# Last layer's first MLP product: pairs of units as seven products of half the features by half the tokens

## The chip, the cores and the metric

The kernel runs on one NeuronCore of a Trainium2 chip. The metric is the device time of one execution in microseconds (us). TensorE (PE) multiplies, ScalarE (ACT) applies functions and copies, VectorE (DVE) does elementwise arithmetic, SyncE (SP) issues the DMA transfers, and PSUM holds what PE writes.

## The reference, cut to what matters

A block with attention, pooling and convolution branches and an MLP is run for two layers. In the last layer only the 512 latent tokens go through the MLP, whose first product (1024 to 4096 features) is what changes:

```python
D_MODEL = 1024
SEQ = 512
D_FF = 4 * D_MODEL

def squared_relu_mlp(h, w1, w2):
    a = jax.nn.relu(h @ w1)
    return (a * a) @ w2

x = x + mod_x[5] * squared_relu_mlp(modulate(rmsnorm(x, g_norm2[l]), mod_x[3], mod_x[4]),
                                    w_ff1[l], w_ff2[l])
```

## The kernel before, in words

Activations lie with features on the 128 partitions and tokens on the free axis: `T` = 768 columns, of which the first 256 (`CT`) are context tokens and unused in the last layer. `h2` is the normalized input of the MLP, eight feature blocks of 128, each as a pair of float32r tiles, high part `hh` and low part `hl`, whose sum is the full value. Every product is made of three terms: weight high by `hh`, weight high by `hl`, weight low by `hh`.

The 4096 hidden features are 32 units of 128. A unit (`ff1`) loads its weights (`wload`: two DMAs of 128x512, each split by an ACT copy into the high part and a DVE subtraction into the low part), runs 8 feature blocks x 3 terms = 24 matmuls into one PSUM tile `mm` (`dense`), and then takes relu (ACT, out of PSUM), square (ACT) and the split into `ah` and `al` (ACT, DVE). The first eight units are done in two parts of 256 tokens, while the normalization of the second part is still under way; the other 24 units use all 512 tokens, so their matmuls have 512 columns. `ff2` multiplies eight units' results by the second weight matrix: 8 output blocks for each of four chunks, each with 24 matmuls of 512 columns and one DVE addition into `x_cur`.

PSUM tiles `mm` have 1024 columns (two halves of 512) and there are two of them in rotation. Weights have four slots in each of two pools (`wf`, `wb`), raw loads six slots in four pools (`rf`, `pd`, `tf`, `rb`). What stands in which order on each engine is not written by hand: `Plan` records every operation with a cost, lays them out in a list by these costs, with the program's dependencies and the slots, and replays them in that order; the tile framework then adds the semaphore waits. In the plan's own bookkeeping a PSUM operand is taken by halves of 512 columns; the framework adds its waits by its own.

All instructions are recorded by one helper, so the profile gives line 352 for every one and is read by tile names.

Of the kernel before, what the change touches and what calls it, by code (L numbers as in the profile page):

```python
# [9 lines left out]
F32 = mybir.dt.float32  # L10
F32R = mybir.dt.float32r
I32 = mybir.dt.int32
AF = mybir.ActivationFunctionType
ALU = mybir.AluOpType
# [3 lines left out]
CT = 256  # L18
T = 768
# [344 lines left out]
def tile_block(ctx, tc, xT, ccol, wmod, cols, rows, wqkv, wcq, wckv, wuq, wukv, wpool,  # L364
# [3 lines left out]
    V, S, PE = _Rec(plan, 'DVE', nc.vector), _Rec(plan, 'ACT', nc.scalar), _Rec(plan, 'PE', nc.tensor)  # L368
    G, SP = _Rec(plan, 'POOL', nc.gpsimd), _Rec(plan, 'SP', nc.sync)
# [8 lines left out]
    rbp = pool("rb", NB['rb'])  # L378
    rfp = pool("rf", NB['rf'])
    wbp = pool("wb", NB['wb'])  # L380
    wfp = pool("wf", NB['wf'])
    epool = pool("e", NB['e'])
    tpool = pool("tmp", NB['tmp'])
    tfp = pool("tf", NB['tf'])
    pdp = pool("pd", NB['pd'])
    stp = pool("st", 3)
    nwp = pool("nw", 1)
    mcp = pool("mc", 1)
    wmp = pool("wm", 2)
# [8 lines left out]
    def nm(s):  # L398
        uid[0] += 1
        return f"{s}_{uid[0]}"  # L400

    def g_tile(shape=(128, T), n="g"):
        return gpool.tile(list(shape), F32R, tag="g", name=nm(n))

    def tmp(shape=(128, T), n="tmp"):
        return tpool.tile(list(shape), F32, tag="tmp", name=nm(n))
# [7 lines left out]
    def mm():  # L414
        return pmm.tile([128, 1024], F32, tag="mm", name=nm("mm"))
# [40 lines left out]
    def split_to(hi, lo, src):  # L456
        S.activation(hi, src, AF.Copy)
        V.tensor_tensor(out=lo, in0=src, in1=hi, op=ALU.subtract)
# [71 lines left out]
    def mod_chunk(l, ch):  # L530


        nv = 2 if l < DEPTH - 1 or ch < 2 else 1
        for hf in range(4):
            acc = mcp.tile([128, 2, 256], F32, tag="mc", name=nm("macc"))
            for k2 in range(8):
                raw = wmp.tile([128, 1, 256], F32, tag="wm", name=nm("wm"))
                j0 = ch * 1024 + hf * 256
                SP.dma_start(raw[:, 0], wmod[l, k2 * 128:(k2 + 1) * 128, j0:j0 + 256])
                for k in range(1):  # L540
                    kt = k2 + k
                    for v in range(nv):
                        if kt == 0:
                            if TOG[2]:
                                S.activation(acc[:, v], raw[:, k], AF.Copy, scale=silu[:, kt, v:v + 1])
                            else:
                                V.tensor_scalar(acc[:, v], raw[:, k], silu[:, kt, v:v + 1], None, op0=ALU.mult)
                        else:
                            V.scalar_tensor_tensor(out=acc[:, v], in0=raw[:, k], scalar=silu[:, kt, v:v + 1], in1=acc[:, v],
                                                   op0=ALU.mult, op1=ALU.add)  # L550
                if k2 == 3:
                    yield
            pt = pst(512)
            for v in range(nv):
                for j in range(2):
                    PE.transpose(pt[:, v * 256 + j * 128:v * 256 + (j + 1) * 128], acc[:, v, j * 128:(j + 1) * 128], ident)
            for v in range(nv):
                V.tensor_reduce(mods[l][:, 8 * ch + 2 * hf:8 * ch + 2 * hf + 2, v],
                                pt[:, v * 256:(v + 1) * 256].rearrange("p (a b) -> p a b", b=128), axis=AX.X, op=ALU.add)
            if hf == 3:  # L560
                mod_bias(l, ch, nv)
            yield
# [14 lines left out]
    def segs(full):  # L577
        return ([(0, CT, 1)] if full else []) + [(CT, T, 0)]
# [10 lines left out]
    def etile():  # L589
        return epool.tile([128, T], F32, tag="e", name=nm("e"))  # L590
# [51 lines left out]
    def tables(l):  # L642
        rw = tmp((128, NROW), "rw")
        SP.dma_start(rw, rows[l:l + 1, :].partition_broadcast(128))
        ra = tmp((128, 2, 6, 64), "ra")
        SP.dma_start(ra, rope_a)
        rb = tmp((128, 2, 6, 32), "rb")
        SP.dma_start(rb, rope_b)
        V.tensor_scalar(rw[:, R_GQA:R_GQA + 64], rw[:, R_GQA:R_GQA + 64], 0.125, None, op0=ALU.mult)
        V.tensor_scalar(rw[:, R_GQB:R_GQB + 96], rw[:, R_GQB:R_GQB + 96], float(96 ** -0.5), None, op0=ALU.mult)  # L650
        for tc_, ts_, ro, gains, hd in ((TAC, TAS, ra, (R_GQA, R_GKA), 32), (TBC, TBS, rb, (R_GQB + 64, R_GKB + 64), 16)):
            for i, r0 in enumerate(gains):
                def bc(o, n, nt):
                    return rw[:, r0 + o:r0 + o + n].unsqueeze(1).to_broadcast([128, nt, n])
                V.tensor_tensor(out=tc_[:, i], in0=ro[:, 0], in1=bc(0, 2 * hd, 6), op=ALU.mult)
                V.tensor_tensor(out=ts_[:, i, :, 0:hd], in0=ro[:, 1, 2:6, 0:hd], in1=bc(hd, hd, 4), op=ALU.mult)
                V.tensor_tensor(out=ts_[:, i, :, hd:2 * hd], in0=ro[:, 1, 2:6, hd:2 * hd], in1=bc(0, hd, 4), op=ALU.mult)
        V.tensor_tensor(out=gno, in0=rw[:, R_GQB:R_GQB + 64], in1=rw[:, R_GKB:R_GKB + 64], op=ALU.mult)
        sm = st()
        for i in range(2):  # L660
            a = R_LAM + 128 * i
            V.tensor_tensor(out=rw[:, a:a + 64], in0=rw[:, a:a + 64], in1=rw[:, a + 64:a + 128], op=ALU.mult)
            V.tensor_reduce(sm[:, i:i + 1], rw[:, a:a + 64], axis=AX.X, op=ALU.add)
        S.activation(sm[:, 2:4], sm[:, 0:2], AF.Exp)
        li = 0.8 - 0.6 * math.exp(-0.3 * l)
        V.tensor_scalar(neglam, sm[:, 3:4], sm[:, 2:3], -li, op0=ALU.subtract, op1=ALU.add)
# [487 lines left out]
    x_cur = []  # L1154
# [13 lines left out]
    for hf, v in ((0, 0), (0, 1), (1, 0), (1, 1)):  # L1168
# [5 lines left out]
        a, b, _ = segs(True)[1 - v]  # L1174
# [4 lines left out]
    for l in range(DEPTH):  # L1179
        full = l < DEPTH - 1  # L1180
# [10 lines left out]
        x_cur = []  # L1191
# [33 lines left out]
        for hp in range(2):  # L1225
            q = a_qk(l, h1, hp, 0, do_fill)
            k = a_qk(l, h1, hp, 1, do_fill)
# [8 lines left out]
        for g in range(2):  # L1236
            q = b_q(l, cq, g, do_fill)
            for i in range(2):
                k, v = b_kv(l, ckv, 2 * g + i, do_fill)
# [16 lines left out]
        for ni, n in enumerate(order):  # L1256
# [14 lines left out]
            for dp in range(4):  # L1271
# [3 lines left out]
                for dd in range(2):  # L1275
                    d = 2 * dp + dd
# [5 lines left out]
                    ps = mm()  # L1282
# [23 lines left out]
        h2 = None  # L1306
        kept = {}
        later = []

        def step():  # L1310

            if later:
                later.pop(0)()
# [8 lines left out]
        for pi, (a, b, v) in enumerate(parts):  # L1322
            for d in (range(8) if pi == 0 else range(7, -1, -1)):
                hi, lo = wkeep(d, wo[l, d], pi)
                ps = mm()
                dense(ps, hi.rearrange("p (k c) -> p k c", c=128), lo.rearrange("p (k c) -> p k c", c=128), 0, mrg, [parts[pi]])
                if pi == 0:
# [3 lines left out]
                                       in1=x_cur[d][:, a:b], op0=ALU.mult, op1=ALU.add)  # L1331
# [3 lines left out]
            h2 = h2 or h_tiles()  # L1335
# [7 lines left out]
        def ff1(f, seg, pi=1):  # L1343
            hi, lo = wkeep(f, wff1[l, f], pi)
            ps = mm()
            dense(ps, hi.rearrange("p (k c) -> p k c", c=128), lo.rearrange("p (k c) -> p k c", c=128), 0, h2, seg)
            a0, a1 = min(x[0] for x in seg), max(x[1] for x in seg)
            a = tmp()
            S.activation(a[:, a0:a1], ps[:, CT + a0:CT + a1], AF.Relu)
            S.activation(a[:, a0:a1], a[:, a0:a1], AF.Square)  # L1350
            if f not in acts:
                acts[f] = (g_tile(n="ah"), g_tile(n="al"))
            split_to(acts[f][0][:, a0:a1], acts[f][1][:, a0:a1], a[:, a0:a1])
            mod_step()
# [3 lines left out]
        def ff2(c, d, seg, pi=1):  # L1358
            hi, lo = wkeep(d, wff2[l, c, d], pi)
            ps = mm()  # L1360
            dense(ps, hi.rearrange("p (k c) -> p k c", c=128), lo.rearrange("p (k c) -> p k c", c=128), 0,
                  [acts[8 * c + k] for k in range(8)], seg)
            for a, b, v_ in seg:
                V.scalar_tensor_tensor(out=x_cur[d][:, a:b], in0=ps[:, CT + a:CT + b], scalar=mods[l][:, 40 + d, v_:v_ + 1],
                                       in1=x_cur[d][:, a:b], op0=ALU.mult, op1=ALU.add)
                if c == 3 and full:
                    acc_square(x_cur[d], ss, d == (0, 7)[pi], a, b)
            mod_step()
            if c == 3 and not full:
                SP.dma_start(out[d], x_cur[d][:, CT:])  # L1370

        if full:
            modq.extend([mod_chunk(l + 1, ch) for ch in range(6)])
        for pi, part in enumerate(parts):
            for f in (range(8) if pi == 0 else range(7, -1, -1)):
                ff1(f, [part], pi)
                step()
        for c in range(3):
            if full and c == 1:
                tables(l + 1)  # L1380
            for f in range(2):
                ff1(8 * (c + 1) + f, segs(full))
            for d in range(8):
                ff2(c, d, segs(full))
            for f in range(2, 8):
                ff1(8 * (c + 1) + f, segs(full))
        if not full:
            for d in range(8):
                ff2(3, d, segs(full))
# [98 lines left out]
```

## Time and profile before

| | us |
|---|---|
| median of 3 runs | 2675.24 (2673.6 to 2675.96) |
| profiled execution, whole | 2676.63 |
| its span, first to last instruction | 2674.9 |
| PE busy in it | 2643.3 (99%) |
| DVE busy | 1754.0 (66%) |
| ACT busy | 1172.6 (44%) |

The sum in the prediction is made on the profiled execution, whose time is 1.7 us over its span and 1.4 us over the median. Busy time of PE is from the start to the modelled end of its matmuls, which overlap; how long one really takes is read from the distance of their starts.

### The profile page before, as it was taken

How to read it: one execution, taken by the hardware profiler on the slowest of the kernel's cores; microseconds unless marked ns; L12 is line 12 of the kernel's file. 1: busy time of each engine (PE TensorE's matmuls, PEld its weight loads, DVE VectorE, ACT ScalarE, POOL GpSimd, SP SyncE). 2: the span in 40 equal slices, each digit the busy share in tenths (PEclk: the TensorE clock that was granted, in tenths of full speed). 3: DMA queues.
4: the chain of work that ended last, by engine and by line, in shares of the span. 5: the costliest groups of instructions: out<-in, count | busy, mean ns of one | idle time of the engine just before them, and what ended most of it. 6: DMA issues, size and time to landing. Idle time of an engine off the chain costs nothing.

```text
span 2674.9 us, 41960 instructions
## 1 busy us (share of the span) xinstructions
PE 2643.3 (99%) x15620; PEld 2310.8 (86%) x15620; DVE 1754.0 (66%) x3978; ACT 1172.6 (44%) x2444; POOL 13.4 (1%) x63
## 2 busy tenths in 40 slices
PE   8999999999999999999999999999999999999999
PEld 4899888989988888988888888888888888988887
DVE  6668666689986778445455467787467887743332
ACT  4355443446564225414141434555455562544332
POOL 0000000000000000000000000000000000000000
PEclk9999999999999999999999999999999999999999
DMA  7222233334446643333444422223232366433332
GB/s 245 77 62 68 87 99 118 96 119 121 130 131 205 213 132 111 103 94 105 127 132 129 127 92 88 72 69 109 89 102 75 94 210 204 147 112 102 95 95 79
DMA packets 189533, 311.90 MB, mean 117 GB/s; under 512 B 21520, under 2 KB 72080, under 8 KB 189328
## 3 DMA queue, kind: packets, MB, share of 16 engines
q1 hardware_dynamic: 189328, 309.22, 37.4%
q8 instruction: 123, 2.02, 0.3%
q14 instruction: 82, 0.67, 0.1%
HBM read 270.86 MB, written 38.27 MB: 116 GB/s over the span
## 4 chain that ended last, share of the span: by engine, by line
PE 92%; DVE 3%; DMA 3%; ACT 1%; issue 1%; SPq 0%; DVEq 0%; ACTq 0%
PE mm L352 79%; PE pst L352 8%; PE sc L352 4%; DMA wmp<-in_wmod_dram 1%; DMA tmp<-y 1%; ACT wh L352 0%; DVE wl L352 0%; DMA wr<-in_wqkv_dram 0%; DVE hl L352 0%; DVE e L352 0%; DMA wm<-in_wmod_dram 0%; DVE ks L352 0%; DVE qd L352 0%; DVE st L352 0%; PE R L352 0%
## 5 line engine op out<-in xcount | busy, mean ns | idle before, releaser
L352 ACT ACTIVATE wh<-wr 128x512 fp32r<-128x512 f32 (+2 forms) x664 | 396.8, 618 | 733.3 <-PE mm L352 608.8
L352 PE MATMUL mm<-hh,wh 128*128 128x256 f32 (+1 forms) x1984 | 613.2, 354 | 2.2 <-DVE xx L352 1.0
L352 PE MATMUL mm<-hh,wl 128*128 128x256 f32 (+1 forms) x1984 | 611.3, 353 | 0.7 <-DVE wl L352 0.6
L352 PE MATMUL mm<-hl,wh 128*128 128x256 f32 (+1 forms) x1984 | 609.7, 353 | 0.0
L352 DVE TENSOR_TENSOR wl<-wr,wh 128x512 fp32r<-128x512 f32 (+2 forms) x664 | 441.7, 676 | 216.6 <-ACT wh L352 210.3
L352 PEld LDWEIGHTS mm<-hh,wl 128*128 128x128 f32 x1984 | 371.4, 189 | 46.4 <-DVE wl L352 1.1
L352 PEld LDWEIGHTS mm<-hh,wh 128*128 128x128 f32 x1984 | 370.6, 189 | 47.2 <-ACT gt L352 1.2
L352 PEld LDWEIGHTS mm<-hl,wh 128*128 128x128 f32 x1984 | 370.7, 189 | 45.5
L352 DVE SCALAR_TENSOR_TENSOR macc<-wm,silu,macc 128x256 f32<-128x256 f32 x448 | 206.1, 481 | 99.3 <-DMA wm<-in_wmod_dram 94.4
L352 PE MATMUL mm<-ah,wh 128*128 128x512 f32 (+1 forms) x768 | 241.9, 355 | 0.4 <-ACT wh L352 0.3
L352 PE MATMUL mm<-al,wh 128*128 128x512 f32 (+1 forms) x768 | 241.8, 355 | 0.0
L352 PE MATMUL mm<-ah,wl 128*128 128x512 f32 (+1 forms) x768 | 241.1, 355 | 0.0
L352 DVE SCALAR_TENSOR_TENSOR xx<-mm,mod,xx 128x256 f32<-128x256 f32 (+1 forms) x96 | 61.3, 660 | 169.7 <-PE mm L352 169.6
L352 ACT ACTIVATE ph<-pst 128x384 fp32r<-128x384 f32 (+1 forms) x216 | 103.2, 478 | 140.8 <-PE pst L352 139.9
L352 PEld LDWEIGHTS mm<-ah,wh 128*128 128x128 f32 x768 | 144.5, 188 | 21.7 <-ACT wh L352 0.8
L352 PEld LDWEIGHTS mm<-al,wh 128*128 128x128 f32 x768 | 144.5, 188 | 21.1 <-issue 0.2
L352 PEld LDWEIGHTS mm<-ah,wl 128*128 128x128 f32 x768 | 144.4, 188 | 20.8 <-issue 0.2
L352 ACT ACTIVATE e<-sc,st 128x768 f32<-128x768 f32 (+1 forms) x160 | 130.5, 815 | 70.9 <-DVE st L352 47.5
L352 PE MATMUL mm<-wh,hh 128*128 128x256 f32 x544 | 154.6, 288 | 2.1 <-ACT wh L352 1.4
L352 PE MATMUL mm<-wl,hh 128*128 128x256 f32 x544 | 154.6, 286 | 0.9 <-DVE wl L352 0.9
L352 PE MATMUL mm<-wh,hl 128*128 128x256 f32 x544 | 153.9, 285 | 0.0
L352 DVE TENSOR_REDUCE st<-sc 128x1 f32<-128x768 f32 (+1 forms) x160 | 135.5, 847 | 19.5 <-PE sc L352 17.0
(196 smaller groups left out, 4579.1 us busy)
## 6 DMA issues: line engine op xcount, KB each, us to landing
wr<-in_wff_dram SPq DMA_DIRECT2D x280, 256.0 KB, 3.0
wr<-in_wdense_dram SPq DMA_DIRECT2D x192, 256.0 KB, 3.0
wm<-in_wmod_dram SPq DMA_DIRECT2D x320, 128.0 KB, 2.2
wr<-in_wbr_dram SPq DMA_DIRECT2D x64, 256.0 KB, 3.6
wr<-in_wqkv_dram SPq DMA_DIRECT2D x48, 256.0 KB, 2.8
g<-gt SPq DMA_DIRECT2D x32, 384.0 KB, 2.6
gt<-g SPq DMA_DIRECT2D x32, 384.0 KB, 3.5
wr<-in_wo_dram SPq DMA_DIRECT2D x48, 256.0 KB, 3.0
```

The lines of the kernel that those rows point to most:

```text
L352: ins = fn(*a, **k).ins
```

## The change

In the last layer the 24 units after the first eight are done in pairs (f, f + 1). A pair is a product of 2 x 2 blocks: the weights are split by unit and by half of the input features (feature blocks 0 to 3 and 4 to 7), the activations by half of the input features and half of the tokens (`lo_t` 256 to 511, `hi_t` 512 to 767). Eight block products become seven, of sums of blocks. `form_sums` makes four sums of activation blocks once: three go where there is room (`t1`, `t2` in the unused context columns of `h2`, `t3` in tiles of other pools) and the fourth is kept in `x_cur` until `form_last` writes it over the block '12'. Each `product` has 4 feature blocks x 3 terms = 12 matmuls of 256 columns into a quarter of a PSUM tile, `pa` or `pb`; `form_w` splits a raw weight block or a sum of them into high and low part. In `ff1_pair` seven sums combine the products into the two units' results, which then take relu, square and split. The order of the calls in a chunk also changes: one pair, six `ff2`, one pair, two `ff2`, two pairs, in place of two units, eight `ff2`, six units.

```diff
+        def form_sums(i, keep4):
+            b11, b12, b21, b22 = (tuple(y[:, t] for y in h2[d]) for d, t in ((i, lo_t), (i, hi_t), (i + 4, lo_t), (i + 4, hi_t)))
+            t1, t2 = (tuple(y[:, free_t] for y in h2[d]) for d in (i, i + 4))
...
+            for dst, b in ((f22, b22), (f12, b12), (f11, b11)):
+                V.tensor_tensor(out=dst, in0=b[0].bitcast(F32), in1=b[1].bitcast(F32), op=ALU.add)
+            V.tensor_tensor(out=t3f, in0=f22, in1=f12, op=ALU.subtract)
+            split_blocks(t3, t3f)
+            V.tensor_tensor(out=f12, in0=f12, in1=f11, op=ALU.subtract)
+            split_blocks(t1, f12)
+            V.tensor_tensor(out=f11, in0=t3f, in1=f11, op=ALU.add)
+            split_blocks(t2, f11)
+            V.tensor_tensor(out=keep4, in0=b21[0].bitcast(F32), in1=b21[1].bitcast(F32), op=ALU.add)
+            V.tensor_tensor(out=keep4, in0=keep4, in1=f11, op=ALU.subtract)
...
+        def form_last(i, keep4):
+            split_blocks(forms['12', i], keep4)
...
+        def product(ps, w, key):
+            for kt in range(4):
+                bh, bl = forms[key, kt]
+                wh, wl = w[:, kt * 128:kt * 128 + 128], w[:, 512 + kt * 128:640 + kt * 128]
+                for i, (w_, b_) in enumerate(((wh, bh), (wh, bl), (wl, bh))):
+                    PE.matmul(ps, lhsT=w_, rhs=b_, start=(kt == 0 and i == 0), stop=(kt == 3 and i == 2))
+
+        def ff1_pair(f):
...
+            pa = mm()
+            pb = mm()
+            p1, p7, p4, p3 = (pa[:, a:a + 256] for a in (0, 512, 256, 768))
+            p6, p5, p2 = (pb[:, a:a + 256] for a in (0, 512, 256))
+            sn = etile()
+            s1, s2, s3 = (sn[:, 256 * k:256 * k + 256] for k in range(3))
+            u1, u2 = tmp(), tmp()
+            product(p1, form_w(r11), '11')
+            S.activation(s1, p1, AF.Copy)
+            V.tensor_tensor(out=r21, in0=r11, in1=r21, op=ALU.subtract)
+            product(p7, form_w(r21), '3')
+            w22 = form_w(r22)
+            V.tensor_tensor(out=r22, in0=r22, in1=r21, op=ALU.subtract)
+            product(p6, form_w(r22), '2')
+            V.tensor_tensor(out=s2, in0=p6, in1=s1, op=ALU.add)
+            V.tensor_tensor(out=s3, in0=p7, in1=s2, op=ALU.add)
+            V.tensor_tensor(out=r11, in0=r22, in1=r11, op=ALU.add)
+            product(p5, form_w(r11), '1')
+            V.tensor_tensor(out=u2[:, hi_t], in0=p5, in1=s3, op=ALU.add)
+            V.tensor_tensor(out=s2, in0=p5, in1=s2, op=ALU.add)
+            product(p4, w22, '12')
+            V.tensor_tensor(out=u2[:, lo_t], in0=p4, in1=s3, op=ALU.add)
+            w12 = form_w(r12)
+            V.tensor_tensor(out=r12, in0=r12, in1=r22, op=ALU.subtract)
+            product(p3, form_w(r12), '22')
+            V.tensor_tensor(out=u1[:, hi_t], in0=p3, in1=s2, op=ALU.add)
+            product(p2, w12, '21')
+            V.tensor_tensor(out=u1[:, lo_t], in0=p2, in1=s1, op=ALU.add)
...
         for c in range(3):
...
+            else:
+                ff1_pair(8 * (c + 1))
+                for d in range(6):
+                    ff2(c, d, segs(full))
+                ff1_pair(8 * (c + 1) + 2)
+                for d in range(6, 8):
+                    ff2(c, d, segs(full))
+                ff1_pair(8 * (c + 1) + 4)
+                ff1_pair(8 * (c + 1) + 6)
```

What the planner made of it is shown at two places. The first is PE where one product ends and the next begins. Before, in the last layer's MLP, this is the seam of a unit of the first product (`hh`, `hl`) and one of the second (`ah`, `al`):

```order
L352 MATMUL mm_4542<-hh_4376,wl_4539 128x512
L352 MATMUL mm_4542<-hh_4378,wh_4538 128x512
L352 MATMUL mm_4542<-hl_4379,wh_4538 128x512
L352 MATMUL mm_4542<-hh_4378,wl_4539 128x512
L352 MATMUL mm_4550<-ah_4432,wh_4546 128x512 [waits Activation_49]
L352 MATMUL mm_4550<-al_4433,wh_4546 128x512 [waits DVE_49]
L352 MATMUL mm_4550<-ah_4432,wl_4547 128x512
```

Every product has a PSUM tile of its own there. In the changed kernel it is the seam of p1 and p7 of the second pair, both in the tile `mm_4597`; `wsf_4602` and `wsf_4603` are their weights (high and low part in one tile), the names that begin with `t_` hold the sum '3':

```order
L352 MATMUL mm_4597<-hh_4370,wsf_4602 128x256
L352 MATMUL mm_4597<-hl_4371,wsf_4602 128x256
L352 MATMUL mm_4597<-hh_4370,wsf_4602 128x256
L352 MATMUL mm_4597<-t_4187_4426,wsf_4603 128x256 [waits Activation_49]
L352 MATMUL mm_4597<-t_4187_4426,wsf_4603 128x256
L352 MATMUL mm_4597<-t_4187_4426,wsf_4603 128x256 [waits Activation_49]
L352 MATMUL mm_4597<-t_4188_4427,wsf_4603 128x256
L352 MATMUL mm_4597<-t_4189_4428,wsf_4603 128x256
```

The first matmul of p7 waits for ACT (the high part of its weights), and so does the third.

The second place is DVE around the readers of PSUM. Before, a stretch of the second product, where each `mm` tile is read once, whole, behind the low parts of weights to come:

```order
L352 SCALAR_TENSOR_TENSOR xx_4309<-mm_4550,mod_133,xx_4309 128x512 [waits PE_49]
L352 TENSOR_TENSOR wl_4567<-wr_4568,wh_4566 128x512 [waits DMAHW3_49,DVE_49,Activation_49]
L352 TENSOR_TENSOR wl_4567<-wr_4569,wh_4566 128x512 [waits DMAHW0_49,Activation_49]
L352 SCALAR_TENSOR_TENSOR xx_4315<-mm_4555,mod_133,xx_4315 128x512 [waits PE_49]
L352 TENSOR_TENSOR wl_4572<-wr_4573,wh_4571 128x512 [waits DMAHW5_49,Activation_49]
L352 TENSOR_TENSOR wl_4572<-wr_4574,wh_4571 128x512 [waits DMAHW2_49,Activation_49]
```

In the changed kernel, in the same second pair, `e_4599` holds s1, s2 and s3, `mm_4598` is `pb`, and `tmp_4601` is u2:

```order
L352 TENSOR_TENSOR wr_4596<-wr_4596,wr_4595 128x512 [waits DVE_49]
L352 TENSOR_TENSOR wl_4619<-wr_4620,wh_4618 128x512 [waits DMAHW5_49,PE_49,Activation_49]
L352 TENSOR_TENSOR wsf_4608<-wr_4596,wsf_4608 128x512 [waits Activation_49]
L352 TENSOR_TENSOR e_4599<-mm_4598,e_4599 128x256 [waits PE_49]
L352 TENSOR_TENSOR e_4599<-mm_4597,e_4599 128x256 [waits DVE_49]
L352 TENSOR_TENSOR wsf_4632<-wr_4623,wsf_4632 128x512 [waits Activation_49]
L352 TENSOR_TENSOR tmp_4601<-mm_4598,e_4599 128x256 [waits DVE_49,PE_49]
L352 TENSOR_TENSOR e_4599<-mm_4598,e_4599 128x256
```

The sums that read `mm` now stand among the weight splits and weight sums, seven times in a pair, and each reads a quarter of a tile.

## Rows read from the trace of the kernel before

**Rows 1.** The page, busy time of each engine.

```profile
PE 2643.3 (99%) x15620; PEld 2310.8 (86%) x15620; DVE 1754.0 (66%) x3978; ACT 1172.6 (44%) x2444; POOL 13.4 (1%) x63
```

**Rows 2.** Windows of the last stage: length, busy times, clock, DMA.

```profile
core 0: us, PE busy (x) PEld busy (x) DVE busy (x) ACT busy (x) POOL busy (x), PEclk, DMA share, GB/s
2365.00:2440.00 75.00, 75.00 (x338) 62.31 (x338) 28.31 (x44) 26.02 (x48) 0.00 (x0) 1.00 0.34 103
2440.00:2520.00 80.00, 80.00 (x355) 66.24 (x354) 29.30 (x44) 27.44 (x49) 0.00 (x0) 1.00 0.31 98
```

**Rows 3.** The chain of waits, 2290 to 2675: its last matmuls.

```profile
2331.29 339.81 PE mm L352 x1637
```

**Rows 4.** Timeline of PE: first and last of 28 matmuls.

```profile
start us, us, engine line op out<-in xcount [idle before <-releaser]
2439.73 0.39 PE L352 MATMUL mm<-hh,wh 128*128 128x512 f32 x1
...
2445.85 0.39 PE L352 MATMUL mm<-hh,wh 128*128 128x512 f32 x1
```

**Rows 5.** Timeline of PE: first and last of 36 matmuls.

```profile
2359.78 0.28 PE L352 MATMUL mm<-hh,wh 128*128 128x256 f32 x1
...
2363.98 0.28 PE L352 MATMUL mm<-hh,wl 128*128 128x256 f32 x1
```

**Rows 6.** Timeline of DVE: operations without a wait between.

```profile
2330.39 1.29 DVE L352 TENSOR_TENSOR wl<-wr,wh 128x512 fp32r<-128x512 f32 x2
2331.59 0.42 DVE L352 TENSOR_TENSOR al<-tmp,ah 128x256 fp32r<-128x256 f32 x1
2331.93 0.87 DVE L352 SCALAR_TENSOR_TENSOR e<-xx,st,R 128x256 f32<-128x256 f32 x2
```

**Rows 7.** Groups of ACT and DVE operations, 2290 to 2675.

```profile
line engine op names shapes xcount | busy us, mean ns | idle before us <-releasers
L352 ACT ACTIVATE wh<-wr 128x512 fp32r<-128x512 f32 x145 | 87.6, 627 | 198.9 <-PE mm L352 194.6 <-DMA wr<-in_wff_dram 4.2
L352 ACT ACTIVATE tmp<-mm 128x256 f32<-128x256 f32 x16 | 6.0, 372 | 2.2 <-PE mm L352 2.2
L352 DVE TENSOR_TENSOR al<-tmp,ah 128x256 fp32r<-128x256 f32 x16 | 6.8, 423 | 3.0 <-ACT ah L352 2.6
```

**Rows 8.** Groups of DVE operations, 2330 to 2365.

```profile
L352 DVE TENSOR_TENSOR wl<-wr,wh 128x512 fp32r<-128x512 f32 x19 | 13.1, 691 | 7.7 <-ACT wh L352 6.9
L352 DVE TENSOR_TENSOR al<-tmp,ah 128x256 fp32r<-128x256 f32 x12 | 5.1, 423 | 2.9 <-ACT ah L352 2.6
L352 DVE SCALAR_TENSOR_TENSOR hl<-e,mod,hh 128x256 fp32r<-128x256 f32 x8 | 3.8, 482 | 0.3 <-ACT hh L352 0.3
```

**Rows 9.** Timeline: PE ends in PSUM, DVE reads it.

```profile
2296.74 0.38 PE L352 MATMUL pss<-ident,ss 128*128 128x128 f32 x2
2297.16 0.42 DVE L352 TENSOR_REDUCE st<-pss 128x2 f32<-128x256 f32 x1 [0.84 <-PE pss L352]
```

**Rows 10.** Timeline: DVE ends, PE restarts on its result.

```profile
1588.26 0.69 DVE L352 TENSOR_TENSOR wl<-wr,wh 128x512 fp32r<-128x512 f32 x1
1589.01 0.39 PE L352 MATMUL mm<-wl,hh 128*128 128x256 f32 x1 [0.90 <-DVE wl L352]
1589.23 0.28 PE L352 MATMUL mm<-wh,hl 128*128 128x256 f32 x1
```

**Rows 11.** Timeline of PE: two stops before the last stage.

```profile
2271.70 0.39 PE L352 MATMUL mm<-ml,wh 128*128 128x256 f32 x1 [0.17 <-DVE ml L352]
2280.08 0.39 PE L352 MATMUL mm<-mh,wh 128*128 128x256 f32 x1 [1.77 <-ACT wh L352]
```

**Rows 12.** Windows with stops of PE.

```profile
1580.00:1590.00 10.00, 7.18 (x53) 6.13 (x51) 9.89 (x21) 4.84 (x10) 0.00 (x0) 1.00 0.00 1
1590.00:1600.00 10.00, 9.69 (x37) 7.51 (x38) 7.95 (x24) 5.12 (x11) 0.00 (x0) 0.83 0.48 158
2268.00:2284.00 16.00, 13.96 (x108) 13.20 (x107) 10.31 (x18) 7.19 (x14) 0.00 (x0) 1.00 0.43 135
```

More of the change, by code (lines that the diff above doesn't have):

```diff
@@ L1370, in ff2, with split_blocks @@
                 SP.dma_start(out[d], x_cur[d][:, CT:])
+        lo_t, hi_t, free_t = slice(CT, 512), slice(512, T), slice(0, CT)
+        forms = {}
+        def split_blocks(blk, src):
+            split_to(blk[0], blk[1], src)
+        def form_sums(i, keep4):
+            b11, b12, b21, b22 = (tuple(y[:, t] for y in h2[d]) for d, t in ((i, lo_t), (i, hi_t), (i + 4, lo_t), (i + 4, hi_t)))
+            t1, t2 = (tuple(y[:, free_t] for y in h2[d]) for d in (i, i + 4))
+            t3 = own3[i]
+            u = etile()
+            w = etile()
+            f22, f12, f11 = (u[:, 256 * k:256 * k + 256] for k in range(3))
+            t3f = w[:, 0:256]
+            for dst, b in ((f22, b22), (f12, b12), (f11, b11)):
[8 more added lines that the diff above has]
+            V.tensor_tensor(out=keep4, in0=keep4, in1=f11, op=ALU.subtract)
+            for n_, b in (('11', b11), ('12', b12), ('21', b21), ('22', b22), ('1', t1), ('2', t2), ('3', t3)):
+                forms[n_, i] = b
@@ new lines, in form_last, with form_w @@
+        def form_last(i, keep4):
+            split_blocks(forms['12', i], keep4)
+        SRAW = ((rfp, "rf"), (pdp, "pd"), (tfp, "tf"), (rbp, "rb"))
+        sturn = [0]
+        def form_w(raw):
+            wp, wt = ((wfp, "wf"), (wbp, "wb"))[sturn[0] % 2]
+            sturn[0] += 1
+            w = wp.tile([128, 1024], F32R, tag=wt, name=nm("wsf"))
+            split_to(w[:, 0:512], w[:, 512:1024], raw)
+            return w
+        def product(ps, w, key):
[4 more added lines that the diff above has]
+                    PE.matmul(ps, lhsT=w_, rhs=b_, start=(kt == 0 and i == 0), stop=(kt == 3 and i == 2))
@@ new lines, in ff1_pair @@
+        def ff1_pair(f):
+            raws = {}
+            for (key, k, a), (rp, rt) in zip((('11', 0, 0), ('21', 1, 0), ('22', 1, 512), ('12', 0, 512)), SRAW):
+                raws[key] = rp.tile([128, 512], F32, tag=rt, name=nm("wr"))
+                SP.dma_start(raws[key], wff1[l, f + k][:, a:a + 512])
+            r11, r21, r22, r12 = (raws[k] for k in ('11', '21', '22', '12'))
+            pa = mm()
[26 more added lines that the diff above has]
+            V.tensor_tensor(out=u1[:, lo_t], in0=p2, in1=s1, op=ALU.add)
+            for k, u in ((1, u2), (0, u1)):
+                S.activation(u[:, CT:T], u[:, CT:T], AF.Relu)
+                S.activation(u[:, CT:T], u[:, CT:T], AF.Square)
+                acts[f + k] = (g_tile(n="ah"), g_tile(n="al"))
+                split_to(acts[f + k][0][:, CT:T], acts[f + k][1][:, CT:T], u[:, CT:T])
@@ L1372, in tile_block @@
         if full:
             modq.extend([mod_chunk(l + 1, ch) for ch in range(6)])
+        else:
+            keep4 = [x_cur[i][:, free_t] for i in range(4)]
+            t3a = mcp.tile([128, 2, 256], F32R, tag="mc", name=nm("t3"))
+            t3b = [wmp.tile([128, 256], F32R, tag="wm", name=nm("t3")) for _ in range(2)]
+            t3c = [g_tile(n="t3") for _ in range(2)]
+            own3 = [(t3a[:, 0], t3a[:, 1]), tuple(t3b)] + [(x[:, 0:256], x[:, 256:512]) for x in t3c]
         for pi, part in enumerate(parts):
@@ L1377, in tile_block @@
                 step()
-        for c in range(3):
[L1379 to L1386, printed above, removed]
+            if pi == 0 and not full:
+                for i in range(4):
+                    later.append(lambda i=i: form_sums(i, keep4[i]))
+        if not full:
+            for i in range(4):
+                form_last(i, keep4[i])
+        for c in range(3):
+            if full:
+                if c == 1:
+                    tables(l + 1)
+                for f in range(2):
+                    ff1(8 * (c + 1) + f, segs(full))
+                for d in range(8):
+                    ff2(c, d, segs(full))
+                for f in range(2, 8):
+                    ff1(8 * (c + 1) + f, segs(full))
+            else:
+                ff1_pair(8 * (c + 1))
[3 more added lines that the diff above has]
+                for d in range(6, 8):
+                    ff2(c, d, segs(full))
+                ff1_pair(8 * (c + 1) + 4)
+                ff1_pair(8 * (c + 1) + 6)
         if not full:
```

## The prediction, made before the changed kernel ran

> **What bounds the kernel now.** Read the page's busy line first [rows 1]: TensorE (PE) is busy 2643.3 of 2674.9 us, but that is a modelled share over many stages, so go to the stage that the change touches. The stretches by windows [rows 2] show the last layer's MLP: PE never idles, VectorE (DVE) works 28 to 29 of 75 to 80 us and ScalarE (ACT) 26 to 27, and the granted clock is 1.00, the 2.4 GHz level. The chain of waits [rows 3] says the same: its last 340 us are one unbroken run of matmuls. So time is gained here only by issuing fewer PE cycles, and lost by every moment in which PE's queue waits. The spacing of matmuls comes from the timeline, by first and last row of an unbroken run: 512 columns take (2445.85 - 2439.73)/27 = 0.227 us [rows 4], 256 columns (2363.98 - 2359.78)/35 = 0.120 us [rows 5]. The "0.39" and "0.28" in those rows are from start to end; neighbours overlap.
>
> **Removed on PE.** Twelve pairs of units change. A pair was 2 x 24 = 48 matmuls of 512 columns, 48 x 0.227 = 10.88 us. It becomes 7 products x 4 feature blocks x 3 terms = 84 matmuls of 256, 84 x 0.120 = 10.08 us. Each pair gives 0.80 us, all twelve 9.6 us. An eighth of the columns goes, but 256-wide matmuls pay their fixed part twice as often.
>
> **Added on DVE and ACT, beside PE.** DVE's 128x512 operations follow one another every 0.60 us, 256-wide ones every 0.34, scalar_tensor_tensor every 0.39 [rows 6] (starts at 2330.39, two operations on at 2331.59, then at 2331.93). A pair now needs 11 of 512 for weights (7 low parts, 4 sums), 7 of 256 to combine products and 2 of 512 for the low parts of the result: 13 x 0.60 + 7 x 0.34 = 10.2 us, against 6 x 0.60 = 3.6 before. For a chunk of four pairs and eight second-matrix units (each 2 x 0.60 and one of 0.75) that is 41 + 16 = 57 us, beside 4 x 10.1 + 8 x 5.44 = 84 us on PE: it fits beside PE, without much to spare where pairs stand back to back. ACT has 7 high parts, one copy and six result operations a pair, 7 x 0.63 + 0.37 + 6 x 0.63 = 8.6 us at the full durations [rows 7], which fits too. I cost both at nothing beyond the waits below. The weights' DMA is four loads of 256 KB a pair, as before; nothing.
>
> **Added once: the sums of activations.** They are 44 + 4 DVE operations of 256, 16.3 us, put into the last eight first-part units (2330 to 2365). There DVE executes 19 operations of 512, 12 of 256 and twice 8 scalar_tensor_tensor [rows 8], about 19 x 0.60 + 12 x 0.34 + 16 x 0.39 = 22 of 35 us; 13 are free, so some 3 to 4.5 us of this work lies behind the seam. The first product needs only plain tokens and the late sums are used by the last products, so the first pair's PE waits little: between 0 and 4.5 us; I take 0.7.
>
> **Added: waits inside every pair.** This is the large term. The seven products of a pair share two PSUM tiles, `pa` (p1, p7, p4, p3) and `pb` (p6, p5, p2), and the readers take one quarter while PE writes another. The dependencies of the built program are by tile, not by quarter. The order rows of PE show it: the third matmul of p7 carries a second wait on ACT, although its low weights come from DVE and its high weights were waited for two rows above. The count waited for, which the rows don't print, is that of the copy of p1; and that copy waits in turn for the matmul just in front, the second of p7, because PE's counter is raised there and not at the end of p1. So PE stands still for a full round trip: its last matmul must end, ACT must start, read, end, and PE restart, with the whole of PE's queue behind it. The same stands at the third matmul of p5 (for the sum that reads p6, on DVE) and a few matmuls into p3 (for the sum that reads p4, on DVE): three a pair, and two pairs have a fourth (p4, for the reader of p7). In the built program I count 12 on ACT and 26 on DVE whose reader is released by the matmul directly ahead. Before, a PSUM tile holds one product and is read once it is complete, so the trace has no such wait; each leg of it is in other rows.
> - The matmul in front, from start to end: 0.28 [rows 5].
> - PE's end to the reader's start: 2297.16 - (2296.74 + 0.38) = 0.04 [rows 9].
> - The reader: an ACT pass of 256 out of PSUM 0.37, a DVE tensor_tensor of 256 0.42 [rows 7].
> - The reader's end to PE's start: 1589.01 - (1588.26 + 0.69) = 0.06; then the first matmul takes 0.39 and its follower starts 0.22 later in place of 0.12, 0.10 more [rows 10].
> - Less the 0.12 that the matmul would have taken anyway.
>
> That is 0.28 + 0.04 + 0.37 + 0.06 + 0.10 - 0.12 = 0.73 us on ACT and 0.78 on DVE: 12 x 0.73 + 26 x 0.78 = 29.0 us. From below a wait could cost nothing at all (if the reader were done in time), from above 1.77, the longest stop of PE for an operand nearby, the shortest being 0.17 [rows 11]. I keep the leg-by-leg value: it contains nothing that could be hidden, because the reader can't start before the matmul in front of the waiting one has ended.
>
> **The sum.** -9.6 + 0.7 + 29.0 = +20.1 us, on the profiled execution's 2676.6 us, which is 1.4 over the median of 2675.24. On the median: 2695.3 us, +0.75%. Changes under 0.2% (5.4 us) can't be told from none here.
>
> The Trainium skill, "PSUM — Partial Sum Buffer" (PSUM bank collisions raise a hardware error), speaks for the change's layout: engines have to be kept apart by bank and by group of 32 partitions, and each successive product here goes to the other bank of its tile or to the other tile. By that rule the three waits a pair are not needed, and without them the sum would be -8.9. No row of before shows a reader and PE in two halves of one tile; the waits stand in the program all the same, so the sum goes by them.
>
> **Rivals.**
> - *The waits cost nothing.* If the readers are done before PE comes to the waiting matmul, only -9.6 + 0.7 = -8.9 is left: 2666.3 us, faster. For it: ACT and DVE have idle time [rows 2] and start a released operation within 0.04 us [rows 9]. Against: the counts, by which the reader is let go one matmul before PE stops. The change wins only if a stop costs under 9/38 = 0.24 us. Chance 0.07.
> - *DVE is also late.* A reader could find one 512-wide operation ahead of it in DVE's queue: 0.60 more for each of 26, up to 15.6 us. The order rows of DVE show a weight's low part directly ahead of the sum that reads p6. Against: that part's inputs are early, and with its stops a pair lasts 12.4 us, which leaves DVE 2.2 over its 10.2. With half of them held, +28 us: 2703; with all, 2711. Chance 0.12.
> - *The clock falls.* In 1580:1590 PE is busy 7.18 of 10 us with stops of 0.9 us, and in 1590:1600 the granted clock is 0.83; in 2268:2284, with 13.96 of 16 us, it stays 1.00 [rows 12]. By the same busy time, which counts a matmul to its end, a pair would stand still for 3 x 0.5 of 12.4 us and be busy for 0.88 of it, near the second of these (0.87) and far from the first (0.72). One such dip costs 0.17 x 10 = 1.7 us; one in each pair 20 us more: 2716. Chance 0.05. The Trainium skill, "TensorE: Matmul & The Clock Gate" (A second HAM failure mode: psum-queue depth-cycling), has this: short idles between matmul groups that wait on PSUM let the clock swing between its two levels. The first of these two stretches agrees with it, the second does not.
>
> **How the numbers follow.** Forecast 0.76, with a range of its own of 2690 to 2700 (0.65 to 0.85 us a stop, and the first pair between 0 and 2). Adding part of the second and third rival at the top, and a little at the bottom for stops that are cheaper than their legs, the range is 2686 to 2706. Faster 0.06 and within 0.2% 0.02, both from the first rival; slower 0.92.
>
> **What would show it.** Right: the timeline of PE has, in every pair, a matmul with 0.45 to 0.6 us of idle time ahead of it just behind the first matmuls of its product, released by ACT `e` (12 times) and DVE `e` or `tmp` (26 times); 256-wide matmuls stay 0.120 apart otherwise, and the clock stays at 1.00. Wrong: PE runs through the pairs at 0.120 a matmul and the end comes 9 us earlier; or the stops are released by weights (`wsf`) instead, which would mean DVE is the bound; or the clock column falls below 1.00 between 2365 and the end.

## The result, and the profile after

The changed kernel takes 2696.02 us (median of 4 runs, 2694.34 to 2697.55), the kernel before, run beside it, 2675.6 (4 runs, 2673.6 to 2676.89): ratio 1.0076, 95% interval 1.0063 to 1.0089. Forecast were 2695.3 us and a range of 2686 to 2706. The profiled execution took 2697.1 us with a span of 2695.2 and a granted clock of 0.999.

The page's busy line, which answers to [rows 1]: PE's busy time grows by 2.9 us, 2.1 of it ahead of the changed stage. In the stage it is nearly unchanged (365.7 and 366.5 us) although PE's work shrinks, because a matmul in front of or behind a stop counts to its full end. DVE's instructions grow most.

```profile
PE 2646.2 (98%) x16052; PEld 2327.0 (86%) x16052; DVE 1848.5 (69%) x4194; ACT 1203.8 (45%) x2508; POOL 13.4 (0%) x63
```

The windows of the changed stage, which answer to [rows 2] (stretch, length, then PE, PEld, DVE, ACT and POOL busy with instructions, granted clock, DMA share, GB/s):

```profile
2365.00:2440.00 75.00, 71.49 (x407) 62.01 (x406) 49.15 (x85) 32.85 (x62) 0.00 (x0) 1.00 0.31 97
2440.00:2520.00 80.00, 73.92 (x459) 65.58 (x459) 50.28 (x91) 34.60 (x63) 0.00 (x0) 1.00 0.30 93
```

PE, which never idled here, now has 3.5 and 6.1 us of idle time in the two stretches; DVE has risen from 28 to 50 us of 80 and is still free for a third of them; the clock is 1.00. So the loss isn't a slower engine but stops of a fast one. The view of waits of PE from 2340 us to the end names every one of them (total us, times, longest):

```profile
PE mm L352 <- DVE e L352: 7.2, 14, 0.5
PE mm L352 <- DVE tmp L352: 6.2, 12, 0.5
PE mm L352 <- ACT e L352: 5.7, 12, 0.5
```

These are 38 stops, 12 on ACT and 26 on DVE, and the view lists nothing else: none on weights (`wsf`), none on a load. Two shorter delays in the first pair, which it doesn't list, come up with no_sums below. The timeline of the second pair shows how one of each kind comes about (start, duration, instruction, and in brackets the idle time before it and its releaser; rows of DMA queues and of PE's weight loads left out):

```profile
2413.71 0.28 PE L352 MATMUL mm<-hl,wsf 128*128 128x256 f32 x1
2413.83 0.28 PE L352 MATMUL mm<-hh,wsf 128*128 128x256 f32 x1
2413.95 0.40 PE L352 MATMUL mm<-t,wsf 128*128 128x256 f32 x2
...
2414.38 0.38 ACT L352 ACTIVATE e<-mm 128x256 f32<-128x256 f32 x1 [0.69 <-PE mm L352]
...
2414.82 1.45 PE L352 MATMUL mm<-t,wsf 128*128 128x256 f32 x10 [0.47 <-ACT e L352]
...
2416.11 0.28 PE L352 MATMUL mm<-hh,wsf 128*128 128x256 f32 x1
...
2417.67 0.28 PE L352 MATMUL mm<-hl,wsf 128*128 128x256 f32 x1
...
2417.98 0.89 DVE L352 TENSOR_TENSOR e<-mm,e 128x256 f32<-128x256 f32 x2 [0.33 <-PE mm L352]
...
2418.46 0.50 PE L352 MATMUL mm<-hh,wsf 128*128 128x256 f32 x2 [0.52 <-DVE e L352]
...
2418.80 0.28 PE L352 MATMUL mm<-hl,wsf 128*128 128x256 f32 x1
```

Read it as the round trip of the prediction. The last matmul of p1 starts at 2413.83. Two matmuls of p7 follow (`t` is the sum of activations that only p7 reads at this place) and end at 2414.35. Only then, at 2414.38, does ACT begin to copy p1, and 0.06 us after its end at 2414.76 PE starts again, at 2414.82. What it costs is seen from starts alone: the two matmuls from 2413.95 and the ten from 2414.82 bring PE to 2416.11, twelve matmuls in 2.16 us where 12 x 0.120 = 1.44 would do: **0.72 us**. For DVE three matmuls take 2418.80 - 2417.67 = 1.13 in place of 0.36: **0.77 us**. The idle time in brackets, 0.47 and 0.52, is only two thirds of that, since the matmul in front has to drain and the one behind starts slowly.

A stage can be measured more sharply than the whole run. From the first matmul of the norm's R ahead of the last MLP to the start of the last matmul of the program, before and after:

```profile
2304.27 0.59 PE L352 MATMUL R<-e,ones 128*128 128x256 f32 x2
...
2670.70 0.39 PE L352 MATMUL mm<-ah,wl 128*128 128x512 f32 x1
```

```profile
2305.39 0.59 PE L352 MATMUL R<-e,ones 128*128 128x256 f32 x2
...
2691.09 0.39 PE L352 MATMUL mm<-ah,wl 128*128 128x512 f32 x1
```

That is 366.43 us before and 385.70 after, +19.3; all else of the two runs differs by about one us. One wait in the stage stands ahead of the pairs: that of R's later matmuls for DVE, some 35 us before the first pair in the changed kernel, 1.07 us idle in the kernel before and 0.46 after.

```profile
2330.62 0.67 PE L352 MATMUL R<-e,ones 128*128 128x256 f32 x2 [1.07 <-DVE e L352]
```

```profile
2331.96 0.67 PE L352 MATMUL R<-e,ones 128*128 128x256 f32 x2 [0.46 <-DVE e L352]
```

It lies between nearly nothing and 1.28 us (before_256) in the kernels below, so a difference of a microsecond between two stages can come from it alone. The same two rows at the ends were read in every kernel:

| kernel | median us | ratio to before, 95% | stage us | stage against before |
|---|---|---|---|---|
| before | 2675.6 | | 366.43 | |
| changed | 2696.02 | 1.0076 (1.0063 to 1.0089) | 385.70 | +19.3 |
| p7_apart | 2685.02 | 1.0036 (1.0022 to 1.0050) | 375.34 | +8.9 |
| three_tiles | 2666.03 | 0.9965 (0.9952 to 0.9977) | 357.86 | -8.6 |
| alternate | 2672.45 | 0.9990 (0.9981 to 0.9999) | 361.17 | -5.3 |
| before_halves | 2685.31 | 1.0039 (1.0023 to 1.0054) | 377.84 | +11.4 |
| before_256 | 2681.9 | 1.0024 (1.0012 to 1.0037) | 374.38 | +8.0 |
| read_wide | 2703.74 | 1.0109 (1.0092 to 1.0126) | 393.74 | +27.3 |
| no_sums | 2696.64 | 1.0085 (1.0070 to 1.0100) | 384.68 | +18.3 |
| three_tiles_dve | 2671.32 | 0.9983 (0.9973 to 0.9992) | 360.16 | -6.3 |

The first four edited kernels ran beside a kernel before of 2674.93 us, the last four beside one of 2676.85.

### The profile page after: what moved, and what is told of

Same layout as the page of the kernel before. It is cut to its first block, busy times and chain, and to the rows that moved or that the text cites. A ratio compares the mean times of both kernels' runs of the same rounds, so it can differ in the third digit from the quotient of the medians.

```text
span 2695.2 us, 43086 instructions
## 1 busy us (share of the span) xinstructions
PE 2646.2 (98%) x16052; PEld 2327.0 (86%) x16052; DVE 1848.5 (69%) x4194; ACT 1203.8 (45%) x2508; POOL 13.4 (0%) x63
## 4 chain that ended last, share of the span: by engine, by line
PE 92%; DVE 3%; DMA 2%; ACT 1%; issue 1%; SPq 0%; ACTq 0%; DVEq 0%
PE mm L352 80%; PE pst L352 8%; PE sc L352 4%; DMA wmp<-in_wmod_dram 1%; DVE e L352 1%; DVE wl L352 0%; ACT wh L352 0%; DMA tmp<-y 0%; DMA wr<-in_wqkv_dram 0%; DVE tmp L352 0%; DVE hl L352 0%; ACT e L352 0%; DVE ks L352 0%; DVE qd L352 0%; DVE st L352 0%
## 5 line engine op out<-in xcount | busy, mean ns | idle before, releaser
L352 ACT ACTIVATE wh<-wr 128x512 fp32r<-128x512 f32 (+3 forms) x616 | 367.1, 616 | 594.0 <-PE mm L352 466.4
L352 PE MATMUL mm<-hh,wh 128*128 128x512 f32 (+1 forms) x1792 | 538.9, 350 | 2.2 <-DVE xx L352 1.0
L352 PE MATMUL mm<-hh,wl 128*128 128x512 f32 (+1 forms) x1792 | 537.1, 350 | 0.7 <-DVE wl L352 0.6
L352 PE MATMUL mm<-hl,wh 128*128 128x512 f32 (+1 forms) x1792 | 534.8, 349 | 0.0
L352 DVE TENSOR_TENSOR wl<-wr,wh 128x512 fp32r<-128x512 f32 (+3 forms) x616 | 408.8, 673 | 149.3 <-ACT wh L352 131.3
L352 PEld LDWEIGHTS mm<-hh,wh 128*128 128x128 f32 x1792 | 334.9, 189 | 40.0 <-ACT gt L352 1.2
L352 PEld LDWEIGHTS mm<-hh,wl 128*128 128x128 f32 x1792 | 335.4, 189 | 38.9 <-DVE wl L352 1.1
L352 PEld LDWEIGHTS mm<-hl,wh 128*128 128x128 f32 x1792 | 335.0, 189 | 38.0
```

What stands on the lines that cost most here:

```text
L352: ins = fn(*a, **k).ins
```

## The experiments

**Is the stop due to the shared tile, and is it the whole loss?** Two edits of the changed kernel give products tiles of their own, with the same arithmetic. The first moves only p7:

```diff
-            p1, p7, p4, p3 = (pa[:, a:a + 256] for a in (0, 512, 256, 768))
+            pc = psp.tile([128, 1024], F32, tag="s", name=nm("pc"))
+            p1, p4, p3 = (pa[:, a:a + 256] for a in (0, 256, 768))
+            p7 = pc[:, 0:256]
```

> Only p7 moves to a PSUM tile of its own, all else as in the changed kernel. Theory A: the 12 stops released by ACT (copy of p1) go, and the two fourth stops of pairs 4 and 8 (reader of p7); 24 stops on DVE stay. -(12 x 0.73 + 2 x 0.78) = -10.3 us: 2685.7. Rival B (DVE and ACT too busy): no change within 3 us, 2693 to 2699. A rule by banks (stops have nothing to do with the tile): no change, 2696.

Measured: 2685.02 us, and 10.4 us less than the changed kernel in the stage, where 10.3 were expected. PE's waits in the pairs were these, 24 stops in place of 38. The number is the one expected, the kinds are not quite: 23 on DVE where 24 were counted, and one on ACT is left. It stands in the first pair, where the matmul behind p1 goes into `mm` and not into p7's new tile:

```profile
PE mm L352 <- DVE e L352: 6.2, 12, 0.5
PE mm L352 <- DVE tmp L352: 5.7, 11, 0.5
PE mm L352 <- ACT e L352: 0.5, 1, 0.5
```

```profile
2366.55 0.38 PE L352 MATMUL mm<-hh,wsf 128*128 128x256 f32 x1 [0.47 <-ACT e L352]
```

The second edit keeps every reader's tile apart from the product that is being written:

```diff
-            p1, p7, p4, p3 = (pa[:, a:a + 256] for a in (0, 512, 256, 768))
-            p6, p5, p2 = (pb[:, a:a + 256] for a in (0, 512, 256))
+            pc = psp.tile([128, 1024], F32, tag="s", name=nm("pc"))
+            p1, p5 = (pa[:, a:a + 256] for a in (0, 512))
+            p7, p3 = (pc[:, a:a + 256] for a in (0, 512))
+            p6, p4, p2 = (pb[:, a:a + 256] for a in (0, 512, 256))
```

> The seven products of a pair in three PSUM tiles (p1 and p5, p7 and p3, p6 with p4 and p2), so that no product is written into a tile whose reader was let go only one matmul before; the arithmetic is unchanged. Theory A (the stops by tile are the whole loss): all 38 stops of 0.47 to 0.52 us go, 38 x about 0.77 = 29 us, and 2696.0 becomes 2667 (2665 to 2670), faster than before by the 9.6 us of fewer PE cycles. Rival B (DVE and ACT have too much to do in a pair, and the stops only hide it): PE stops on weights (wsf) in their place, and the time is above 2680. Rival C (only the copy of p1 counts, since ACT is slow to begin): the time falls by 12 x 0.73 = 9 us at most, to 2687.

Measured: 2666.03 us, faster than both kernels, 8.9 us under before (ratio 0.9952 to 0.9977). All 38 stops are gone. What is left are two waits for weights in the first pair, 1.2 us together; in the second stretch by windows PE is busy without a gap:

```profile
PE pc L352 <- ACT wsf L352: 1.0, 1, 1.0
PE pc L352 <- DVE wsf L352: 0.2, 1, 0.2
```

```profile
2440.00:2520.00 80.00, 80.00 (x498) 72.48 (x497) 55.65 (x99) 37.04 (x67) 0.00 (x0) 1.00 0.31 100
```

In the same 80 us PE executes 498 matmuls here and 459 in the changed kernel. The timeline shows the reader at work in peace, while PE goes on in another tile (`pc`):

```profile
2412.76 0.28 PE L352 MATMUL mm<-hh,wsf 128*128 128x256 f32 x1
2412.88 0.28 PE L352 MATMUL pc<-hh,wsf 128*128 128x256 f32 x1
2413.00 0.28 PE L352 MATMUL pc<-hl,wsf 128*128 128x256 f32 x1
...
2413.09 0.43 DVE L352 TENSOR_TENSOR tmp<-mm,e 128x256 f32<-128x256 f32 x1
2413.12 0.40 PE L352 MATMUL pc<-hh,wsf 128*128 128x256 f32 x2
2413.36 0.28 PE L352 MATMUL pc<-hl,wsf 128*128 128x256 f32 x1
```

**Does it need more PSUM, or only another order?** Two tiles again, but p6 comes ahead of p7, so that products alternate strictly between the tiles:

```diff
-            p1, p7, p4, p3 = (pa[:, a:a + 256] for a in (0, 512, 256, 768))
-            p6, p5, p2 = (pb[:, a:a + 256] for a in (0, 512, 256))
+            p1, p7, p4, p2 = (pa[:, a:a + 256] for a in (0, 512, 256, 768))
+            p6, p5, p3 = (pb[:, a:a + 256] for a in (0, 512, 256))
...
-            product(p7, form_w(r21), '3')
...
             product(p6, form_w(r22), '2')
             V.tensor_tensor(out=s2, in0=p6, in1=s1, op=ALU.add)
+            product(p7, form_w(r21), '3')
```

> Two PSUM tiles as in the changed kernel, but p6 is computed ahead of p7 and successive products alternate strictly between the tiles, so that a reader has one product (12 x 0.120 = 1.44 us) before its tile is written again. Theory A: nearly all stops go without more PSUM, 2667 to 2672 (a stop may be left where a pair follows a pair, since p2 is the first tile's last product and the next pair begins in it: up to 12 x 0.4). Rival B (DVE too busy): the weights of p6 now need both sums first, so PE stops on wsf in every pair: above 2680. A rule by banks: no change, 2696.

Measured: 2672.45 us (11 runs, 2668.47 to 2675.65), 0.1% under before (ratio 0.9981 to 0.9999), which the prediction calls too little to tell from no change, and 0.5 us above the range expected. Another order alone brings 38 stops down to six. Five of the six are in the first pair (2370 to 2382 us):

```profile
PE mm L352 <- DVE tmp L352: 1.4, 3, 0.5
PE mm L352 <- DVE e L352: 1.0, 2, 0.5
PE mm L352 <- ACT e L352: 0.7, 1, 0.7
```

The four on DVE are the same round trip as above and not a late DVE: DVE is idle until the matmul directly ahead of the stop has ended. One of them:

```profile
2378.36 0.28 PE L352 MATMUL mm<-hl,wsf 128*128 128x256 f32 x1
...
2378.67 0.42 DVE L352 TENSOR_TENSOR tmp<-mm,e 128x256 f32<-128x256 f32 x1 [0.26 <-PE mm L352]
...
2379.15 0.51 PE L352 MATMUL mm<-hh,wsf 128*128 128x256 f32 x2 [0.52 <-DVE tmp L352]
```

So in that pair the planner still put readers behind a matmul of the next product in their tile. Why only there, where DVE also has the sums of activations to make, wasn't looked into.

The stage's 3.3 us over three_tiles fit six stops (4.6 us at 0.77) less the 1.2 us that three_tiles waits there. The medians lie 6.4 us apart; the other 3 us are outside the stage, and I leave them open. In the profiled executions the stage begins at 2307.37 us in alternate and at 2300.04 in three_tiles, after work that is the same in both.

**Does the mechanism need the change at all?** The kernel before, with the two units of a pair in the two halves (512 columns each) of one tile:

```diff
+            if f % 2 == 0:
+                both.append(mm())
...
+            p = both[-1][:, 512 * (f % 2):512 * (f % 2) + 512]
```

> The kernel before, with one edit: the two units of a pair take the two halves (two PSUM banks) of one tile, in place of a tile each; 512 columns a matmul, no sums of blocks, DVE and ACT work as before. Theory A: the second unit's first matmuls are followed by one stop a pair, for the reader of the first unit (ACT, 512 wide, out of PSUM): 0.39 + 0.04 + 0.58 + 0.06 + 0.10 - 0.23 = 0.94 us, 12 of them 11.3 us, 2686.9. Theory of banks (two halves of a tile don't touch one another): no change, 2675.6.

Measured: 2685.31 us, +11.4 us in the stage where 11.3 were expected. One stop a pair, 12 in all, of 0.69 us idle, by the waits and by one of them in the timeline:

```profile
PE mm L352 <- ACT tmp L352: 8.2, 12, 0.7
```

```profile
2437.20 0.39 PE L352 MATMUL mm<-hh,wl 128*128 128x512 f32 x1
...
2437.63 0.60 ACT L352 ACTIVATE tmp<-mm 128x512 f32<-128x512 f32 x1 [0.27 <-PE mm L352]
...
2438.28 0.50 PE L352 MATMUL mm<-hh,wh 128*128 128x512 f32 x1 [0.69 <-ACT tmp L352]
2438.62 0.40 PE L352 MATMUL mm<-hl,wh 128*128 128x512 f32 x1
```

By the starts a stop costs 2438.62 - 2437.20 - 2 x 0.227 = 0.97 us, where 0.94 were expected. The second unit writes no column that the reader of the first reads, so this is a wait by tile, without any of the change's sums, narrow matmuls or extra DVE work.

**Is a stop's price the whole round trip?** In the changed kernel the copy of p1 is made longer, and nothing else is:

```diff
-            S.activation(s1, p1, AF.Copy)
+            S.activation(sn.rearrange("p (a b) -> p a b", b=256), p1.unsqueeze(1).to_broadcast([128, 3, 256]), AF.Copy)
```

> The changed kernel with one edit: the ACT copy of p1 reads the quarter three times over and writes 768 columns in place of 256 (the two other copies are overwritten later). Theory A (a stop is a round trip that holds the reader's whole duration): the reader takes 0.37 + 2 x (0.58 - 0.37) = 0.79 in place of 0.37, each of the 12 stops on ACT grows from 0.47 to 0.89 us idle, +5.0 us: 2701. Rival D (a stop's price is PE's own restart, or ACT's start): no change, 2696. Rival B (ACT and DVE too busy): more than 10 us, and stops on weights.

Measured: 2703.74 us, +8.0 us in the stage over the changed kernel, where 5.0 were expected. The reader takes 0.811 us, and the 12 stops on ACT grew from 5.7 to 10.8 us, 0.47 to 0.90 each, as theory A has it:

```profile
PE mm L352 <- ACT e L352: 10.8, 12, 0.9
PE mm L352 <- DVE e L352: 8.3, 16, 0.6
PE mm L352 <- DVE tmp L352: 7.4, 14, 0.9
```

The rest are four more stops on DVE than before, 30 in place of 26 (15.7 - 13.4 = 2.3 us idle, some 3 with their drain and restart), which I hadn't expected. Two of the four are in the first pair, and the fourth and the eighth pair have one more each; none is on weights. That the planner orders the program otherwise for a longer copy is likely but wasn't followed up.

**What do the narrower matmuls cost?** The kernel before, its 24 units in two passes of half the tokens:

```diff
+            for cut in ([[x] for x in seg] if not full and len(seg) == 2 else [seg]):
+                dense(ps, hi.rearrange("p (k c) -> p k c", c=128), lo.rearrange("p (k c) -> p k c", c=128), 0, h2, cut)
...
+            cuts = [(CT, 512, 0), (512, T, 0)]
...
+                ff1(8 * (c + 1) + f, segs(full) if full else cuts)
```

> The kernel before, its 24 first-matrix units of the changed stage computed in two passes of 256 tokens each, 48 matmuls in place of 24 a unit: the same columns, twice the instructions, no sums and no shared tiles. Theory A (a 256-wide matmul takes 0.120, not half of 0.227): 24 x (48 x 0.120 - 24 x 0.227) = +7.5 us, 2682.4. Rival (width is free, only columns count): no change, 2675. Rival (twice the weight loads bind PE): over 2690.

Measured: 2681.9 us (ratio 1.0012 to 1.0037) and +8.0 us in the stage, where 7.5 were expected. From 2340 us on PE doesn't stop once; the timeline has the 256-wide matmuls 0.120 apart, (2440.04 - 2439.80)/2:

```profile
2439.80 0.28 PE L352 MATMUL mm<-hh,wh 128*128 128x256 f32 x1
2439.92 0.28 PE L352 MATMUL mm<-hl,wh 128*128 128x256 f32 x1
2440.04 0.28 PE L352 MATMUL mm<-hh,wl 128*128 128x256 f32 x1
```

So seven products of eight save 12.5% of the columns of a pair and 0.80/10.88 = 7.4% of its time; the narrower matmuls take back the other 5%.

**Are the sums of activations hidden?**

```diff
-            for dst, b in ((f22, b22), (f12, b12), (f11, b11)):
-                V.tensor_tensor(out=dst, in0=b[0].bitcast(F32), in1=b[1].bitcast(F32), op=ALU.add)
...
-            split_blocks(forms['12', i], keep4)
```

> The changed kernel without the 48 DVE operations that form the sums of activation blocks (and their ACT passes): the products take plain blocks instead; same products, weights, readers and tiles. Theory A (all of this work is hidden in the changed kernel, since the first stops give DVE and ACT time to catch up): within 1.3 us of 2696. Rival E (the seam costs up to 4.5 us): 2691.5 to 2694.

Measured: 2696.64 us, no gain. In the stage it is 1.0 us shorter. Half of that is the wait of 0.5 us for R, which the changed kernel has and this one hardly has; the 38 stops have the same totals. The other half stands in the first pair of the changed kernel, in two delays too short for the view of waits:

```profile
2369.07 0.28 PE L352 MATMUL mm<-hl,wsf 128*128 128x256 f32 x1
2369.36 0.50 PE L352 MATMUL mm<-t,wsf 128*128 128x256 f32 x2
2369.70 0.40 PE L352 MATMUL mm<-hh,wsf 128*128 128x256 f32 x2
...
2371.76 0.69 DVE L352 TENSOR_TENSOR wsf<-wr,wsf 128x512 fp32r<-128x512 f32 x1
...
2372.22 0.78 PE L352 MATMUL mm<-hh,wsf 128*128 128x256 f32 x3
2372.84 0.28 PE L352 MATMUL mm<-hl,wsf 128*128 128x256 f32 x1
```

Three matmuls take 0.63 and 0.62 us there in place of 0.36, 0.5 us too much in all. The second delay ends as DVE has made a low part of weights (2371.76 + 0.69 = 2372.45). Without the sums, the first pair has its three stops and no such delay.

**Is DVE at its limit?** three_tiles, with two more operations of 256 columns for each product, whose results nobody uses:

```diff
         def product(ps, w, key):
+            for d in (4, 6):
+                V.tensor_tensor(out=x_cur[d][:, free_t], in0=forms[key, 0][0].bitcast(F32), in1=forms[key, 0][1].bitcast(F32), op=ALU.add)
```

> The kernel with three PSUM tiles a pair and two more DVE operations of 256 columns for each product, whose results nobody uses: 14 x 0.34 = 4.8 us a pair, so DVE needs 15.0 us a pair where PE needs 10.1; a chunk asks 41 + 19 + 16 = 76 us of DVE in 84. Theory A (DVE works ahead during the second-matrix units, and its load isn't what the changed kernel loses by): under 8 us more than three tiles alone, 2666 to 2674, the stops where three pairs follow one another. Rival B (in a pair DVE is at its limit): each pair lasts what DVE needs, up to 12 x 4.9 = 59 us more, 2700 to 2725.

Measured: 2671.32 us, inside what theory A gave; the stage is 2.3 us longer than in three_tiles. DVE is busy for 76 of 80 us, and PE has no gap:

```profile
2440.00:2520.00 80.00, 80.00 (x498) 72.47 (x498) 76.06 (x164) 38.56 (x69) 0.00 (x0) 1.00 0.33 102
```

PE waits for 2.7 us in all, for weights, all of it before 2380 us. DVE's load was not what the changed kernel lost by, with room for 4.8 us more a pair.

## Why the prediction was right

- **PE's work, -9.6 us.** Right. In the changed kernel 256-wide matmuls stay 0.120 apart outside the stops, and with the stops away three_tiles comes to 2666.03 us, where the first rival (-9.6 + 0.7) had 2666.3. That the two agree this closely is partly luck: three_tiles still waits 1.2 us for weights, and hasn't the 1.07 us that the kernel before waits for R.
- **Stops, +29.0 us.** Right in number, kind and size; number and kind had been counted in the built program. 12 on ACT and 26 on DVE, 0.72 and 0.77 us in place of 0.73 and 0.78, so 12 x 0.72 + 26 x 0.77 = 28.7. That they are due to the tile is shown both ways: they go with separate tiles (p7_apart, three_tiles) and come with a shared one in a kernel that has nothing else of the change (before_halves). That the price contains the reader's whole duration is shown by read_wide.
- **The first pair, +0.7 us.** Right in size: two short delays, 0.5 us together, which no_sums hasn't. Without the stops the lateness shows more, as 1.2 us of waits for weights in three_tiles; so part of it is most likely covered by the stops, in which DVE and ACT catch up, which the prediction did not say.
- **The extra work of DVE and ACT at nothing.** Right but for that 0.5 us: none of the 38 stops was released by weights, and three_tiles_dve has DVE at 95% of a stretch with PE unhindered. So the second rival (DVE also late, 2703 to 2711) fell: all 26 stops on DVE are 0.52 us, none has another operation's 0.60 in it.
- **The clock.** The third rival fell too: 1.00 in every stretch with three stops a pair, as in the second of the two stretches of [rows 12]. The stops in the first of them, 0.9 us as in [rows 10], waited for results of DVE and were not waits on PSUM, so that stretch was a weak model for this kernel.
- **The first rival** (the waits cost nothing) fell in the changed kernel. It had a rule on its side, that engines have to be kept apart by bank and by group of 32 partitions (Trainium skill, "PSUM — Partial Sum Buffer", PSUM bank collisions raise a hardware error). before_halves shows that this program waits for more than that rule asks: two banks of one tile, and still 12 stops of 0.69 us idle, because the program's own dependencies go by tile. Whether the chip would bear reader and writer in two banks of one tile without that wait wasn't tried, since the wait can't be taken away alone.

The account of the stage closes: -9.6 + 28.7 + 0.5 = 19.6, less 0.6 for the shorter wait for R, which no term foresaw, is 19.0, and 19.3 were measured. The medians lie 20.4 us apart, nearer to the 20.1 of the forecast than the stage is: about one us of that lies outside the stage and is luck.

## What to carry to other kernels

Before several results share one PSUM tile, ask at each of them who still reads the tile when the next matmul writes it: a reader that is let go by the matmul directly ahead of the writer costs PE the whole round trip, drain, reader and restart, here 0.7 to 0.8 us for readers of 0.4. Count such pairs of reader and writer in the built program, and price each by its legs from rows that are already there. What helped here was a third tile (all stops gone) or the same tiles in alternation with one whole product between write and read (six stops left). And a saving in columns is worth less than its share where it makes matmuls narrower: an eighth was 7.4% here.

## What was not expected of the hardware

In three_tiles_dve DVE was busy for 76 of 80 us and PE did not stand still in that stretch; how far ahead the weights were formed was not read. And the drain and the slow first matmul around a stop are a third of its price. The prediction had both legs in its sum, but whoever reads only a profile's idle column, 0.47 and 0.52 us, understates a stop.
